# Convolution module of a two-layer trunk: the last gate ahead of the first tile's transposes, silu by pairs of blocks, and sixteen identity products behind the second tile's transposes

## The chip, the cores and the metric

The kernel runs on one core of one Trainium2 chip. The metric is the device time of one execution in microseconds (us). Changes are judged by the median over runs on the same chip.

## The reference, cut to what matters

Two layers follow each other. Each is a half-step SwiGLU FFN, a token mixer, and a second half-step FFN, all with norms before and after and a residual. The mixer of layer 0 is a causal convolution module; the change touches only this one. With 256 tokens and 1024 channels it computes:

```python
def conformer_conv_module(x, w_in, b_in, w_dw, b_dw, ln_g, ln_b, w_out, b_out):
    a, gate = jnp.split(x @ w_in + b_in, 2, axis=-1)
    h = a * jax.nn.sigmoid(gate)
    h = lax.conv_general_dilated(
        h, w_dw[:, None, :].astype(h.dtype),
        window_strides=(1,), padding=[(CONV_WIDTH - 1, 0)],
        dimension_numbers=("NWC", "WIO", "NWC"),
        feature_group_count=D_MODEL) + b_dw
    h = jax.nn.silu(layer_norm(h, ln_g, ln_b))
    return h @ w_out + b_out
```

## The kernel before

The 256 tokens are two tiles of 128 rows, t = 0 and t = 1. The 1024 channels of the convolution are four chunks of 256, c = 0 to 3. All products are done in three parts: a float32 operand is split into a high part (ACT casts it, L136) and a low part (DVE subtracts, L137), and three matmuls sum high by high, high by low and low by high (`mm3`, L139 to L142). Weights come from HBM in pieces of 512 KB on SP's queue (L127) and are split in the same way, so ACT and DVE carry a steady load of weight splits beside the module's own work.

`conv_mixer` works in these steps for each tile t and chunk c:

- `gate(t, c)`: 24 matmuls of 512 columns (`project`, L291 to L295) into a PSUM tile `mm`; DVE adds the bias (L488), ACT takes the sigmoid (L491), DVE multiplies (L493), and the result is split into `lg`.
- `conv(t, c)`: the convolution by a Fourier transform along the tokens. Six matmuls (twelve for t = 1, which needs the tile before as well) bring the chunk to the spectrum, in a PSUM tile `tr`. DVE multiplies with the taps' spectrum (five instructions, L513 to L517), the product is split into `cc`, and six matmuls bring it back into another `tr`; DVE adds the bias (L526) and takes batch statistics (L527).
- `norm(t)`: when all four chunks of a tile are there, DVE joins the statistics (L531), POOL makes the reciprocal root (L151, L155), and DVE normalises the tile in two halves (L536).
- `turn(t, z)`: the normalised tile is transposed in two halves of four blocks each (PE, L546) into two `tr` tiles. ACT applies the layer norm's gain and bias to each block (L553) and takes a sigmoid (L557), DVE multiplies (L558), and the result is split into `xt`. In the first half this goes by pairs of blocks (256 columns), in the second by all four (512).
- the output product: `expand` (L303) makes 48 matmuls of 512 columns for a tile into two `acc` tiles, and `post_norm` adds to the residual.

PSUM has four `acc` tiles, two `mm` and two `tr`; a new `tr` takes the buffer of the last but one, and its first writer waits until that one has been read. The code states the work in a program order; a scheduler decides at build time the order in which each engine's queue holds it, and fills in work that stands further down in the code. On the chip each engine runs its queue. The order around the change is this, in the code:

```python
        for t, c in ((0, 0), (1, 0), (0, 1), (1, 1), (0, 2)):
...
        sa = turn(0, za)
        conv(1, 3)
...
        sbt = turn(1, norm(1))
        accs = [[acc(), acc()] for _ in range(NT)]
        expand(accs[0], blocks(*sa, KD), wo, True, True)
        post_norm(0, accs[0], gain, 1.0, b_out)
```

The second tile's `expand` and its `post_norm` are handed on as `rest`, and run inside the start of the next FFN, whose `pre_norm` transposes the residual (L175). `behind(pe)` (L113) is a helper that makes the instructions told inside it come after the last instruction told so far on that engine.

Of the kernel before, what the change touches and what calls it, by code (L numbers as in the profile page):

```python
# [11 lines left out]
AF = mybir.ActivationFunctionType  # L12
ALU = mybir.AluOpType
# [3 lines left out]
P = 128  # L17
D = 1024
ROOT = 32.0
KD = D // P  # L20
FF = 2816
CH = 256
# [18 lines left out]
def trunk_kernel(  # L41
# [39 lines left out]
    def acc():  # L81
        return new(ps, [P, 512], F32, "acc", 4)
# [4 lines left out]
    def tr():  # L87
        return new(ps, [P, 512], F32, "tr", 2)
# [209 lines left out]
    def blocks(hi, lo, n):  # L298
        if len(hi.shape) == 3:
            return [(hi[:, k], lo[:, k]) for k in range(n)]  # L300
        return [(hi[:, k * P : (k + 1) * P], lo[:, k * P : (k + 1) * P]) for k in range(n)]
# [169 lines left out]
    def conv_mixer(layer, spectrum, before):  # L471
# [4 lines left out]
        xt = start(base, before)  # L476
        hc = [b4() for _ in range(NT)]
        stats = [new(sb, [P, 4, 6], F32, "stats", 2) for _ in range(NT)]
        glu = {}
        ws = {}  # L480

        def gate(t, c):
# [12 lines left out]
            split(hl[:, :CH], hl[:, CH:], h)  # L495
            glu[t, c] = hl

        def conv(t, c):
            sl = slice(c * CH, (c + 1) * CH)
            u = tr()  # L500
            srcs = [(glu[t, c], C_FWD)]
            if t > 0:
                srcs.append((glu[t - 1, c], C_HIS))
            for part in range(2):
                for i, (hl, off) in enumerate(srcs):
                    cs = slice(off + part * NH, off + (part + 1) * NH)
                    mm3(u[:NH, part * CH : (part + 1) * CH], dh[:, cs], dl[:, cs],
                        hl[:, :CH], hl[:, CH:], i == 0, i == len(srcs) - 1)
            wri = wspec[c // 2][:NH, c % 2 * 512 : c % 2 * 512 + 512]
            wr, wi = wri[:, :CH], wri[:, CH:]  # L510
            m1, m2 = wide("ca"), wide("cb")
            y = m1
            dve.tensor_tensor(m1[:NH], u[:NH, :], wri, op=ALU.mult)  # L513
            dve.tensor_tensor(m2[:NH, :CH], u[:NH, :CH], wi, op=ALU.mult)
            dve.tensor_tensor(m2[:NH, CH:], u[:NH, CH:], wr, op=ALU.mult)
            dve.tensor_tensor(y[:NH, :CH], m1[:NH, :CH], m1[:NH, CH:], op=ALU.subtract)
            dve.tensor_tensor(y[:NH, CH:], m2[:NH, :CH], m2[:NH, CH:], op=ALU.add)  # L517
            yh, yl = wide("cc", F32R), wide("cc", F32R)
            split(yh[:NH], yl[:NH], y[:NH])
            v = tr()  # L520
            for part in range(2):
                cs = slice(C_INV + part * P, C_INV + (part + 1) * P)
                ys = slice(part * CH, (part + 1) * CH)
                mm3(v[:, :CH], dh[:NH, cs], dl[:NH, cs], yh[:NH, ys], yl[:NH, ys],
                    part == 0, part == 1)
            dve.tensor_tensor(hc[t][:, sl], v[:, :CH], b_dw[:, sl], op=ALU.add)  # L526
            dve.bn_stats(stats[t][:, c, :], hc[t][:, sl])  # L527
# [9 lines left out]
                                  op0=ALU.subtract, op1=ALU.mult)  # L537
            return z

        def turn(t, z):  # L540
            hi, lo = turned(t)
            for h in range(2):
                pt = tr()
                for j in range(4):
                    k = h * 4 + j
                    pe.transpose(pt[:, j * P : (j + 1) * P], z[:, k * P : (k + 1) * P], ident)  # L546
                y, s = hc[t][:, h * 512 : (h + 1) * 512], z[:, h * 512 : (h + 1) * 512]
                for j in range(4):
                    k = h * 4 + j
                    js = slice(j * P, (j + 1) * P)  # L550
                    g = gcol[:, G_LN + k : G_LN + k + 1]
                    b = gcol[:, G_LN + KD + k : G_LN + KD + k + 1]
                    act.activation(y[:, js], pt[:, js], AF.Identity, scale=g, bias=b)  # L553
                step = 256 if h == 0 else 512
                for a in range(0, 512, step):
                    bs = slice(a, a + step)
                    act.activation(s[:, bs], y[:, bs], AF.Sigmoid)  # L557
                    dve.tensor_tensor(y[:, bs], y[:, bs], s[:, bs], op=ALU.mult)  # L558
                    ks = slice((h * 512 + a) // P, (h * 512 + a + step) // P)
                    split(hi[:, ks], lo[:, ks], y[:, bs].rearrange("p (k m) -> p k m", m=P))  # L560
            return hi, lo

        for t, c in ((0, 0), (1, 0), (0, 1), (1, 1), (0, 2)):
            gate(t, c)
            conv(t, c)
        gate(0, 3)
        conv(0, 3)
        za = norm(0)
        gate(1, 2)
        conv(1, 2)  # L570
        gate(1, 3)
        sa = turn(0, za)
        conv(1, 3)
        b_out = row(V_BOUT)
        gain = row(V_POST + base)
        wo = [weight(True) for _ in range(8)]
        sbt = turn(1, norm(1))
        accs = [[acc(), acc()] for _ in range(NT)]
        expand(accs[0], blocks(*sa, KD), wo, True, True)
        post_norm(0, accs[0], gain, 1.0, b_out)  # L580

# [361 lines left out]
```

## Time and profile before

| | |
|---|---|
| Median of three runs | 1009.26 us (1008.78 to 1009.34) |
| The profiled execution | 1008.88 us, of which 1007.0 us is the span from the first to the last instruction |
| PE busy | 99% of the span |
| DVE busy | 74% |
| ACT busy | 54% |
| Mean granted TensorE clock | 0.995 of full speed |

The span is what the trace shows; 1.88 us lie outside of it. PE is TensorE's matmuls, DVE is VectorE, ACT is ScalarE, POOL is GpSimd. The convolution module occupies roughly 199 to 293 us of the span.

### The profile page before, as it was taken

To read this page: it belongs to the slowest core of one execution; us is meant where nothing else is said; L and a number is where in the kernel's file an instruction comes from. 1 tells how busy PE (TensorE), PEld (TensorE's weight loads), DVE (VectorE), ACT (ScalarE), POOL (GpSimd) and SP (SyncE) were. 2 spreads that over 40 slices of the span, in tenths; PEclk is the share of its full clock that TensorE was granted. 3 is DMA by queue.
4 is the path that set the end of the run, shared out by engine and by line. 5 is a ranking of instruction groups with operands and counts; after the bars stand their busy time and mean duration, and the time that the engine had idled before them with its cause. 6 is when DMAs were issued, how large, how long until landed. Compare 5 with 4: busy or idle time off the path is not lost.

```text
span 1007.0 us, 14787 instructions
## 1 busy us (share of the span) xinstructions
PE 992.5 (99%) x5412; PEld 854.8 (85%) x5412; DVE 749.7 (74%) x1274; ACT 548.6 (54%) x1000; POOL 53.6 (5%) x93
## 2 busy tenths in 40 slices
PE   9999999999899999999999999999999999999997
PEld 7888888888778888888888888889998888888886
DVE  6877667799887776767776767687788596767673
ACT  6656545764485555455755554584143385555541
POOL 1000000010021000000200000030001120000000
PEclk9999999999899999999999999999999999999999
DMA  7885555642527564646465646465232555555541
GB/s 250 273 279 181 187 198 172 236 179 104 181 96 235 180 219 161 222 160 221 168 198 178 210 166 223 167 208 179 82 126 93 179 195 181 189 187 199 178 147 42
DMA packets 50952, 182.06 MB, mean 181 GB/s; under 512 B 6048, under 2 KB 6176, under 8 KB 50880
## 3 DMA queue, kind: packets, MB, share of 16 engines
q1 hardware_dynamic: 50736, 181.09, 53.4%
q8 instruction: 42, 0.69, 0.3%
q14 instruction: 30, 0.25, 0.1%
q10 hardware_dynamic: 144, 0.03, 0.0%
HBM read 180.06 MB, written 1.05 MB: 180 GB/s over the span
## 4 chain that ended last, share of the span: by engine, by line
PE 94%; DVE 2%; ACT 1%; DMA 1%; POOL 1%; issue 0%; DVEq 0%; POOLq 0%; SPq 0%; ACTq 0%
PE tr L331 14%; PE mm L331 14%; PE acc L141 9%; PE acc L140 9%; PE acc L142 9%; PE tr L333 7%; PE mm L333 7%; PE mm L291 4%; PE mm L292 4%; PE mm L295 4%; PE tr L654 2%; PE mm L351 2%; PE mm L352 2%; PE mm L350 2%; DMA raw<-wts 1%; PE tr L175 1%
## 5 line engine op out<-in xcount | busy, mean ns | idle before, releaser
L137 DVE TENSOR_TENSOR wl<-raw,wh 128x1024 fp32r<-128x1024 f32 (+1 forms) x386 | 399.9, 1059 | 89.1 <-ACT wh L136 65.0
L136 ACT CAST wh<-raw 128x1024 fp32r<-128x1024 f32 (+1 forms) x386 | 340.4, 921 | 124.7 <-DMA raw<-wts 72.3
L331 PE MATMUL mm<-xt,wh 128*128 128x512 f32 x640 | 161.6, 393 | 0.5 <-ACT wh L136 0.5
L331 PE MATMUL tr<-xt,wh 128*128 128x512 f32 x640 | 160.7, 392 | 0.0
L140 PE MATMUL acc<-wh,b 128*128 128x512 f32 x352 | 138.0, 392 | 0.0
L141 PE MATMUL acc<-wl,b 128*128 128x512 f32 x352 | 137.4, 390 | 0.0
L331 PEld LDWEIGHTS mm<-xt,wh 128*128 128x128 f32 x640 | 116.9, 188 | 24.1 <-ACT wh L136 1.3
L142 PE MATMUL acc<-wh,b 128*128 128x512 f32 x352 | 137.0, 389 | 0.0
L331 PEld LDWEIGHTS tr<-xt,wh 128*128 128x128 f32 x640 | 115.0, 189 | 20.7
L333 PEld LDWEIGHTS mm<-xt,wl 128*128 128x128 f32 x640 | 87.5, 190 | 6.7 <-DVE wl L137 0.4
L333 PEld LDWEIGHTS tr<-xt,wl 128*128 128x128 f32 x640 | 87.3, 190 | 6.2
L333 PE MATMUL mm<-xt,wl 128*128 128x256 f32 x640 | 90.0, 282 | 0.2 <-DVE wl L137 0.2
L333 PE MATMUL tr<-xt,wl 128*128 128x256 f32 x640 | 89.2, 282 | 0.0
L136 ACT CAST b<-e 128x256 fp32r<-128x256 f32 x80 | 32.5, 406 | 95.8 <-DVE e L412 95.8
L142 PEld LDWEIGHTS acc<-wh,b 128*128 128x128 f32 x352 | 66.1, 188 | 14.1
L140 PEld LDWEIGHTS acc<-wh,b 128*128 128x128 f32 x352 | 66.2, 188 | 12.6
L141 PEld LDWEIGHTS acc<-wl,b 128*128 128x128 f32 x352 | 66.2, 188 | 12.2
L336 ACT COPY e<-tr 128x256 f32<-128x256 f32 x80 | 29.4, 368 | 85.1 <-PE tr L333 85.1
L337 DVE TENSOR_TENSOR ga<-tr,e 128x256 f32<-128x256 f32 x80 | 33.7, 421 | 55.6 <-ACT e L336 55.6
L291 PE MATMUL mm<-wh,xt 128*128 128x512 f32 x176 | 70.0, 398 | 0.0
L292 PE MATMUL mm<-wl,xt 128*128 128x512 f32 x176 | 69.2, 393 | 0.0
L336 ACT COPY e<-mm 128x256 f32<-128x256 f32 x80 | 29.7, 371 | 49.0 <-PE mm L333 48.8
(180 smaller groups left out, 1251.9 us busy)
## 6 DMA issues: line engine op xcount, KB each, us to landing
raw<-wts SPq DMA_DIRECT2D x328, 512.0 KB, 4.8
b<-rows SPq DMA_DIRECT2D x10, 512.0 KB, 6.5
b<-x_turned SPq DMA_DIRECT2D x4, 256.0 KB, 6.3
x<-x_in SPq DMA_DIRECT2D x2, 512.0 KB, 8.4
out_dram<-x SPq DMA_DIRECT2D x4, 256.0 KB, 2.0
b<-dft SPq DMA_DIRECT2D x1, 371.0 KB, 4.8
ca<-masks SPq DMA_DIRECT2D x1, 192.0 KB, 4.5
b<-w_dw SPq DMA_DIRECT2D x1, 128.0 KB, 4.9
```

The lines of the kernel that those rows point to most:

```text
L136: act.copy(dst_h, src)
L137: dve.tensor_tensor(dst_l, src, dst_h.bitcast(F32), op=ALU.subtract)
L140: pe.matmul(o, lh, rh, start=first, stop=False)
L141: pe.matmul(o, lh, rl, start=False, stop=False)
L142: pe.matmul(o, ll, rh, start=False, stop=last)
L291: pe.matmul(o, hi[:, k], wh[:, sl], start=k == 0, stop=False)
L292: pe.matmul(o, hi[:, k], wl[:, sl], start=False, stop=False)
L295: pe.matmul(o, a, w, start=False, stop=h == 1 and n == 3)
L331: pe.matmul(pair, block(ws[k // 2][0], k), xhl[:, k], start=k == 0, stop=False)
L333: pe.matmul(pair[:, 0], block(ws[k // 2][1], k), xhl[:, k, 0], start=False, stop=k == KD - 1)
L336: act.copy(cross, o[:, SEQ:])
L337: dve.tensor_tensor(res[:, part * SEQ : (part + 1) * SEQ], o[:, :SEQ], cross, op=ALU.add)
```

## The change

Three things are edited in `conv_mixer`.

- `conv` is cut in two functions, `spectral` (to the spectrum, the product with the taps, its split) and `back` (the six matmuls back, bias, statistics). In the code `turn(0, za)` now stands behind `gate(1, 3)` and ahead of `back(1, 2)`, where before `conv(1, 2)` was told whole ahead of `gate(1, 3)`. The two DVE products of 256 columns (L514, L515) become one of 512 columns that reads the taps with the halves swapped (L513 of the changed kernel).
- In `turn` both halves go by pairs: gain and bias for two blocks, then their sigmoid, product and split, then the next two. Before, the gain and bias of all four blocks stood ahead.
- Behind the second tile's transposes sixteen products of the identity with itself are told, into `accs[1][0]`, which the second tile's `expand` overwrites later. For this the four `acc` tiles are made ahead of `turn(1, ...)`.

```diff
-        def conv(t, c):
-            sl = slice(c * CH, (c + 1) * CH)
+        def spectral(t, c):
             u = tr()
...
-            dve.tensor_tensor(m2[:NH, :CH], u[:NH, :CH], wi, op=ALU.mult)
-            dve.tensor_tensor(m2[:NH, CH:], u[:NH, CH:], wr, op=ALU.mult)
+            dve.tensor_tensor(m2[:NH].rearrange("p (s n) -> p s n", s=2),
+                              u[:NH].rearrange("p (s n) -> p s n", s=2),
+                              wri.rearrange("p (s n) -> p s n", s=2)[:, ::-1, :], op=ALU.mult)
...
             split(yh[:NH], yl[:NH], y[:NH])
+            prod[t, c] = yh, yl
+
+        def back(t, c):
+            yh, yl = prod.pop((t, c))
+            sl = slice(c * CH, (c + 1) * CH)
             v = tr()
...
-        def turn(t, z):
+        def turn(t, z, spare=None):
...
+                if spare is not None and h == 1:
+                    with behind(pe):
+                        for j in range(16):
+                            pe.matmul(spare[:, j % 4 * P : (j % 4 + 1) * P], ident, ident, start=True, stop=True)
                 y, s = hc[t][:, h * 512 : (h + 1) * 512], z[:, h * 512 : (h + 1) * 512]
-                for j in range(4):
...
-                    act.activation(y[:, js], pt[:, js], AF.Identity, scale=g, bias=b)
-                step = 256 if h == 0 else 512
-                for a in range(0, 512, step):
-                    bs = slice(a, a + step)
+                for a in range(0, 512, 256):
+                    bs = slice(a, a + 256)
+                    ks = slice((h * 512 + a) // P, (h * 512 + a + 256) // P)
+                    for j in range(a // P, a // P + 2):
...
+                        act.activation(y[:, js], pt[:, js], AF.Identity, scale=g, bias=b)
                     act.activation(s[:, bs], y[:, bs], AF.Sigmoid)
                     dve.tensor_tensor(y[:, bs], y[:, bs], s[:, bs], op=ALU.mult)
...
         za = norm(0)
         gate(1, 2)
-        conv(1, 2)
+        spectral(1, 2)
         gate(1, 3)
         sa = turn(0, za)
-        conv(1, 3)
+        back(1, 2)
+        spectral(1, 3)
+        back(1, 3)
         b_out = row(V_BOUT)
         gain = row(V_POST + base)
         wo = [weight(True) for _ in range(8)]
-        sbt = turn(1, norm(1))
         accs = [[acc(), acc()] for _ in range(NT)]
+        sbt = turn(1, norm(1), accs[1][0])
         expand(accs[0], blocks(*sa, KD), wo, True, True)
```

What the scheduler makes of it is seen at three places. The first is PE's queue at the end of `gate(1, 3)` (L295, into `mm`); `tr` from `cc` is a product back, `tr` from `ident` a transpose, `tr` from `lg` a product to the spectrum. Before:

```order
L295 MATMUL mm_2650<-wh_2507,xt 128x512 x2
L140 MATMUL tr_2641<-cc_2637,b_177_921 128x256
L546 MATMUL tr_2684<-ident,b_527_2580 128x128 x4
L141 MATMUL tr_2641<-cc_2638,b_177_921 128x256
L142 MATMUL tr_2641<-cc_2637,b_178_922 128x256
L140 MATMUL tr_2641<-cc_2637,b_177_921 128x256
L141 MATMUL tr_2641<-cc_2638,b_177_921 128x256
L142 MATMUL tr_2641<-cc_2637,b_178_922 128x256
L546 MATMUL tr_2701<-ident,b_527_2580 128x128 x4
L140 MATMUL tr_2714<-lg_2681,b_177_921 81x256
```

The same place now:

```order
L295 MATMUL mm_2634<-wh_2502,xt 128x512 x2
L551 MATMUL tr_2668<-ident,b_527_2574 128x128 x4
L551 MATMUL tr_2685<-ident,b_527_2574 128x128 x4
L140 MATMUL tr_2702<-cc_2630,b_177_921 128x256
L141 MATMUL tr_2702<-cc_2631,b_177_921 128x256
L142 MATMUL tr_2702<-cc_2630,b_178_922 128x256
L140 MATMUL tr_2702<-cc_2630,b_177_921 128x256
L141 MATMUL tr_2702<-cc_2631,b_177_921 128x256
L142 MATMUL tr_2702<-cc_2630,b_178_922 128x256
L140 MATMUL tr_2711<-lg_2665,b_177_921 81x256
```

Both groups of transposes have moved ahead of the whole of `back(1, 2)`. Its `tr_2702` now takes the buffer of the first transposes (`tr_2668`), and `spectral(1, 3)` with `tr_2711` that of the second (`tr_2685`).

The second place is PE's queue at the end of `spectral(1, 3)`. Before, the first tile's `expand` (`acc` from `wh` and `wl`) stands right behind it:

```order
L142 MATMUL tr_2714<-lg_2544,b_178_922 81x256
L140 MATMUL acc_2854<-wh_2753,xt 128x512
L141 MATMUL acc_2854<-wl_2754,xt 128x512
L140 MATMUL acc_2855<-wh_2753,xt 128x512
L142 MATMUL acc_2854<-wh_2753,xt 128x512
L141 MATMUL acc_2855<-wl_2754,xt 128x512
```

Further down its queue, 22 matmuls of the 48 stand ahead of the first matmul of `back(1, 3)` and 42 ahead of the second tile's transposes. Now:

```order
L142 MATMUL tr_2711<-lg_2539,b_178_922 81x256
L140 MATMUL tr_2734<-cc_2730,b_177_921 128x256
L141 MATMUL tr_2734<-cc_2731,b_177_921 128x256
L142 MATMUL tr_2734<-cc_2730,b_178_922 128x256
L140 MATMUL tr_2734<-cc_2730,b_177_921 128x256
L141 MATMUL tr_2734<-cc_2731,b_177_921 128x256
L142 MATMUL tr_2734<-cc_2730,b_178_922 128x256
L551 MATMUL tr_2824<-ident,b_585_2821 128x128 x4
L551 MATMUL tr_2841<-ident,b_585_2821 128x128 x4
L555 MATMUL acc_2813<-ident 128x128 x16
L140 MATMUL acc_2811<-wh_2749,xt 128x512
```

All 48 matmuls of the first tile's `expand` have moved behind `back(1, 3)`, the second tile's transposes and the sixteen identity products; the second tile's 48 follow, with the next FFN's transposes (L175) behind fifteen of them.

The third place is ACT's queue at the same point as the first. Before:

```order
L136 CAST wh_2809<-raw_2807 128x512 x2
L491 ACTIVATE e_2677<-ga_2675 128x256
L136 CAST cc_2637<-ca_2630 81x512
L136 CAST lg_2681<-e_2679 128x256
L553 ACTIVATE b_406_2064<-tr_2684,gcol 128x128 x4
L557 ACTIVATE b_527_2580<-b_406_2064 128x256 x2
```

Now:

```order
L136 CAST wh_2805<-raw_2803 128x512 x2
L565 ACTIVATE b_406_2064<-tr_2668,gcol 128x128 x2
L491 ACTIVATE e_2661<-ga_2659 128x256
L136 CAST cc_2630<-ca_2624 81x512
L566 ACTIVATE b_527_2574<-b_406_2064 128x256
L136 CAST lg_2665<-e_2663 128x256
L565 ACTIVATE b_406_2064<-tr_2668,gcol 128x128 x2
L565 ACTIVATE b_406_2064<-tr_2685,gcol 128x128
L136 CAST xt<-b_406_2064 128x2x128
L566 ACTIVATE b_527_2574<-b_406_2064 128x256
L565 ACTIVATE b_406_2064<-tr_2685,gcol 128x128 x2
L566 ACTIVATE b_527_2574<-b_406_2064 128x256
```

The reading of the transposes is now woven into the gate's and the spectrum's work; one more L565 of `tr_2685` follows. DVE's queue between `spectral(1, 3)` and the second tile's transposes holds what it held before, the weight splits among it, with the two products L514 and L515 as one.

## Rows read from the trace of the kernel before

**Rows 1.** The page's first part: busy us and share of each engine.

```profile
PE 992.5 (99%) x5412; PEld 854.8 (85%) x5412; DVE 749.7 (74%) x1274; ACT 548.6 (54%) x1000; POOL 53.6 (5%) x93
```

**Rows 2.** Busy time by stretch around the transposes, with granted clock as PEclk.

```profile
256.52:259.24 2.72, 0.01 (x1) 0.01 (x1) 2.72 (x7) 1.86 (x4) 0.00 (x0) 1.00 1.00 387
259.24:266.60 7.36, 7.18 (x30) 6.33 (x31) 6.20 (x15) 6.76 (x18) 0.00 (x0) 0.54 0.36 128
280.18:292.93 12.75, 12.18 (x56) 9.82 (x57) 11.13 (x24) 10.94 (x27) 0.85 (x2) 1.00 0.19 66
```

**Rows 3.** PE in order of time: start, us; in brackets idle before it, releaser.

```profile
255.44 1.08 PE L295 MATMUL mm<-wh,xt 128*128 128x512 f32 x4
259.24 0.39 PE L140 MATMUL tr<-cc,b 81*128 81x256 f32 x1 [2.72 <-ACT cc L136]
...
262.84 0.41 PE L141 MATMUL tr<-lg,b 128*81 128x256 f32 x1
...
264.97 0.41 PE L142 MATMUL tr<-lg,b 128*81 128x256 f32 x1
...
272.68 0.28 PE L142 MATMUL tr<-cc,b 81*128 81x256 f32 x1
...
276.67 1.11 PE L546 MATMUL tr<-ident,b 128*128 128x128 f32 x8 [0.29 <-DVE b L536]
277.54 0.47 PE L140 MATMUL acc<-wh,xt 128*128 128x512 f32 x1
...
285.12 0.66 PE L175 MATMUL tr<-ident,x 128*128 128x128 f32 x4 [0.57 <-DVE x L279]
...
286.57 0.40 PE L142 MATMUL acc<-wh,xt 128*128 128x512 f32 x1
...
292.70 0.39 PE L142 MATMUL acc<-wh,xt 128*128 128x512 f32 x1
292.93 0.39 PE L291 MATMUL mm<-wh,xt 128*128 128x512 f32 x1
...
296.66 0.66 PE L175 MATMUL tr<-ident,x 128*128 128x128 f32 x4 [0.62 <-DVE x L279]
```

**Rows 4.** DVE in order of time, at the first and the second tile's norm.

```profile
254.31 1.01 DVE L536 TENSOR_SCALAR b<-b,tiny,tiny 128x512 f32<-128x512 f32 x2 [0.71 <-POOL tiny L155]
...
255.83 0.68 DVE L513 TENSOR_TENSOR ca<-tr,b 81x512 f32<-81x512 f32 x1
256.43 0.41 DVE L514 TENSOR_TENSOR cb<-tr,b 81x256 f32<-81x256 f32 x1
256.76 0.41 DVE L515 TENSOR_TENSOR cb<-tr,b 81x256 f32<-81x256 f32 x1
...
274.87 0.25 DVE L531 BATCH_NORM_AGGREGATE tiny<-stats 128x2 f32<-128x24 f32 x1
276.07 1.00 DVE L536 TENSOR_SCALAR b<-b,tiny,tiny 128x512 f32<-128x512 f32 x2 [0.95 <-POOL tiny L155]
```

**Rows 5.** ACT in order of time, from the last weight cast to the first sigmoids.

```profile
256.32 1.14 ACT L136 CAST wh<-raw 128x512 fp32r<-128x512 f32 x2 [2.83 <-DMA raw<-wts]
258.26 0.42 ACT L491 ACTIVATE e<-ga 128x256 f32<-128x256 f32 x1 [0.80 <-DVE ga L488]
258.58 0.60 ACT L136 CAST cc<-ca 81x512 fp32r<-81x512 f32 x1
...
260.15 1.51 ACT L553 ACTIVATE b<-tr,gcol 128x128 f32<-128x128 f32 x4 [0.28 <-PE tr L546]
261.54 0.73 ACT L557 ACTIVATE b<-b 128x256 f32<-128x256 f32 x2
```

**Rows 6.** PE: identity products at the program's start, other products of their size later.

```profile
1.50 5.49 PE L202 MATMUL tr<-ident 128*128 128x128 f32 x24 [1.50 <-POOL ident masks.py:199]
...
742.59 1.05 PE L639 MATMUL tr<-b,b 128*128 128x128 f32 x8
743.40 0.48 PE L291 MATMUL mm<-wh,xt 128*128 128x512 f32 x1
```

More of the change, by code (lines that the diff above doesn't have):

```diff
@@ L478, in conv_mixer @@
         stats = [new(sb, [P, 4, 6], F32, "stats", 2) for _ in range(NT)]
-        glu = {}
+        glu, prod = {}, {}
         ws = {}
@@ L546, in turn @@
                     pe.transpose(pt[:, j * P : (j + 1) * P], z[:, k * P : (k + 1) * P], ident)
+                if spare is not None and h == 1:
+                    with behind(pe):
+                        for j in range(16):
+                            pe.matmul(spare[:, j % 4 * P : (j % 4 + 1) * P], ident, ident, start=True, stop=True)
                 y, s = hc[t][:, h * 512 : (h + 1) * 512], z[:, h * 512 : (h + 1) * 512]
-                for j in range(4):
[L549 to L552, printed above, removed]
-                    act.activation(y[:, js], pt[:, js], AF.Identity, scale=g, bias=b)
-                step = 256 if h == 0 else 512
-                for a in range(0, 512, step):
-                    bs = slice(a, a + step)
+                for a in range(0, 512, 256):
+                    bs = slice(a, a + 256)
+                    ks = slice((h * 512 + a) // P, (h * 512 + a + 256) // P)
+                    for j in range(a // P, a // P + 2):
+                        k = h * 4 + j
+                        js = slice(j * P, (j + 1) * P)
+                        g = gcol[:, G_LN + k : G_LN + k + 1]
+                        b = gcol[:, G_LN + KD + k : G_LN + KD + k + 1]
+                        act.activation(y[:, js], pt[:, js], AF.Identity, scale=g, bias=b)
                     act.activation(s[:, bs], y[:, bs], AF.Sigmoid)
                     dve.tensor_tensor(y[:, bs], y[:, bs], s[:, bs], op=ALU.mult)
-                    ks = slice((h * 512 + a) // P, (h * 512 + a + step) // P)
                     split(hi[:, ks], lo[:, ks], y[:, bs].rearrange("p (k m) -> p k m", m=P))
             return hi, lo
-        for t, c in ((0, 0), (1, 0), (0, 1), (1, 1), (0, 2)):
+        for t, c in ((0, 0), (1, 0), (0, 1), (1, 1), (0, 2), (0, 3)):
             gate(t, c)
-            conv(t, c)
-        gate(0, 3)
-        conv(0, 3)
+            spectral(t, c)
+            back(t, c)
         za = norm(0)
         gate(1, 2)
-        conv(1, 2)
+        spectral(1, 2)
         gate(1, 3)
         sa = turn(0, za)
-        conv(1, 3)
+        back(1, 2)
+        spectral(1, 3)
+        back(1, 3)
         b_out = row(V_BOUT)
```

## Prediction

> **What bounds the kernel now.** The page comes first: PE is busy for 992.5 of 1007.0 us, so nearly every microsecond at which PE stands still, or runs at the lower clock, is a microsecond of the time [rows 1]. The next view is therefore PE in order of time, searched for idle time. The largest gap behind the program's start lies inside the convolution module, where PE has finished the last gate and waits 2.72 us, up to 259.24, for the split of tile 1's spectrum [rows 3]. The windows show what follows: the granted clock averages 0.54 over the next 7.36 us, so PE runs there mostly at the lower of its two levels, 1.2 GHz instead of 2.4 [rows 2]. The reader should see from the same timeline that PE is then fed without a longer pause: the first tile's output products cover the wait for the product back of the second tile, which comes through at 272.68, and most of the wait for its norm, so that the transposes at 276.67 cost only 0.29 us of idle time [rows 3]. The stage ends for our purpose at 292.93, where the next FFN's first product starts [rows 3].
>
> **What the change moves.** I follow the new queues from the end of the gate at 256.52, 255.44 plus 1.08 [rows 3], and ask at each step which engine is last. The part ahead of it keeps its work and its order but for small swaps, and PE has no gap there that could shrink; I count it at nothing. If the swaps opened gaps there, they would come on top.
>
> *The first transposes.* The normalised tile is written from 254.31 for 1.01 us, done at 255.32 [rows 4], so the eight transposes run at once behind the gate. Eight take 277.54 - 276.67 = 0.87 us at the full clock [rows 3], so PE is through at about 257.3. That much of the 2.72 us is filled.
>
> *The product back, `back(1, 2)`.* It needs the buffer that ACT still reads. ACT is free after two weight casts that start at 256.32 and take 1.04 us of its queue, at 257.36 (steps are from one start to the next, so a little under the busy times) [rows 5]. Its queue then holds two gain-and-bias blocks at (261.54 - 260.15) / 4 = 0.35, the gate's sigmoid at 0.32, the cast of `cc` at 0.52 (the like step of a weight cast), a sigmoid at 0.31, the cast of `lg` at 0.31, and two more blocks at 0.35 [rows 5]: 0.70 + 0.32 + 0.52 + 0.31 + 0.31 + 0.70 = 2.86, and 0.1 for the last one's end. PE gets the buffer at 260.35 and has been idle for 3.05 us, 0.33 more than before. DVE's split of `cc` is ready earlier, near 259.7, since DVE meets one weight split fewer ahead of it and L514 and L515, 0.33 each, cost 0.60 together as one 512-column product like L513 [rows 4]: the saving of 0.06 in a convolution is hidden behind PE everywhere but in this chain.
>
> *The twelve products to the spectrum.* They wait for the buffer of the second transposes: ACT has a block, a cast, a sigmoid, two blocks, a sigmoid and a block still to go, 4 x 0.35 + 3 x 0.31 = 2.33 from 260.21, so they start at about 262.7. With the lower clock they step by (264.97 - 262.84) / 10 = 0.213 [rows 3] and are done at 262.7 + 11 x 0.213 + 0.41 = 265.4, as late as before (264.97 + 0.41).
>
> *The wait for `back(1, 3)`.* Here PE's queue has lost its cover. From 265.45, DVE does L512, a split of `xt` that stands in between, L513, L516, a weight split and L517: 0.60 + 0.34 + 0.60 + 0.34 + 0.60 + 0.41 = 2.89, with 256-column steps as L514's and 512-column ones as L513's [rows 4]. The cast and the way to PE take 0.66, from 258.58 to 259.24 [rows 3, 5]. The first matmul starts at 269.1. The other five need the low half, which stands behind two weight splits: 268.3 + 3 x 0.60 + 0.1 = 270.2. Six matmuls are over at about 271.5. Before, this point was 272.68 + 0.28 = 272.96 [rows 3], so tile 1's chain gains some 1.5 us, and PE has stood idle for 3.7 and 0.7 us of it, where before it made output products.
>
> *The wait for the second transposes.* From there to their start it was 276.67 - 272.96 = 3.71 us before [rows 3], with 1.20 from L531 to L536 through POOL and 0.60 for the first half of L536 in it [rows 4]. DVE's queue holds the same instructions here and three weight splits ahead, which end at 271.9; I take 3.5. The transposes start at 275.0, 1.7 earlier, but PE has idled all the way.
>
> *The identity products.* Twelve of them at the program's start are 24 records in 5.49 us, 0.229 each [rows 6]; sixteen are 32 records. Eight records of the same size elsewhere take 743.40 - 742.59 = 0.81, 0.10 each [rows 6]. So they cost between 3.2 and 7.3 us. After the long gaps I expect the lower clock at the start. Before, the low stretch lasted 7.36 us from PE's resuming [rows 2], and the slow records at the program's start 5.49 [rows 6]. I take 5.2 us here, near the second, where PE also ran without a break: transposes at half pace to 276.6, sixteen records to 280.2, sixteen at 0.11 (0.87 / 8, as the transposes) to 282.0. A low stretch of 7.4 us would give 283.1, one of only 3.4 us 281.0.
>
> *The output products.* Twenty-seven steps from 286.57 to 292.70 take 6.13 us, 0.227 each [rows 3], so 48 take 10.9. All 48 of tile 0 are now behind the identity products: 282.0 + 10.9 = 292.9. Tile 1's 48 follow with the eight transposes of the next FFN (0.95 with the slower neighbours); these need the residual 296.66 - 292.93 = 3.73 after the tile's last product, and fifteen products cover 3.40, so PE waits 0.33, no longer 0.57 [rows 3]. The next FFN starts at 292.9 + 10.9 + 0.95 + 0.33 = 305.1 against 292.93. Its second transposes stand behind twenty products, 4.54 us, and no longer wait 0.62 [rows 3].
>
> **The sum** is +12.2 - 0.6 = +11.6 us. PE is busy all through what follows, so nothing gives it back. The profiled time of 1008.88 becomes 1020.5; the median of the runs shown is 0.38 higher, so I predict 1020.7.
>
> **Where a rule is weighed.** In rows 3 PE waited 0.29 us at 276.67 with six output products behind the transposes whose operands were long there; it did not take them first. The Trainium skill, "TensorE: Matmul & The Clock Gate", section "Part 2: What happens when you issue a matmul", says that only weight loads are pulled ahead and matmuls stay in program order. By that rule the first rival below has no chance, and the trace agrees. On the clock, rows 2 and 3 show it low after a gap of 2.72 us. The same page, section "Part 1: The HAM clock gate", calls the throttled state the default, released by activity, which speaks for identity products in general. By the rule alone they could pay where idle time follows them; here the order puts 48 ready products behind them, and the sum stays that of the rows.
>
> **The rivals.**
> - *PE takes ready products past waiting ones* (faster). Then the idle time is filled again. Work left from 256.52 is 24 matmuls of 256 columns at half of 0.227 (2.7), 24 transposes at 0.109 (2.6), 96 products (21.8) and the identity's 3.5 at the full clock: 30.6 us against 36.4 (292.93 - 256.52), so -5.8 and 1003.5. The 0.29, 0.57 and 0.62 us waits with work behind them speak against it [rows 3]. It decides from the point where idle time falls under 5.8 us. In queue order the bare chains are longer: 3.05 ahead of `back(1, 2)`, 0.60 + 0.60 + 0.34 + 0.41 + 0.66 = 2.6 ahead of `back(1, 3)`, 2.5 ahead of the transposes (3.71 less two weight splits), 8.1 in all, a loss of 2.3 us even at the full clock throughout. Chance 0.03.
> - *The clock stays high, or returns at once.* The gaps are broken by short work. Then the spectrum is done a microsecond earlier, the second transposes start near 273.8, they and the identity products take 0.9 + 3.5, and tile 0's output starts at 278.2 instead of 282.0: +7.8, 1017. The clock held at 1.00 from 280.18 to 292.93, through the wait of 0.57 us [rows 2, 3]; the 2.72 us gap speaks against it. Chance 0.17.
> - *The clock returns later, or the splits in DVE's queue wait for weights still in flight.* One low stretch as long as before's 7.36 us inside the output products, or a transfer 2 us late in the queue ahead of `cc`, gives +14 to +17, 1023 to 1026. ACT did wait 2.83 us for weights here [rows 5], but ahead of this stretch. Chance 0.08.
> - *No measurable change*: the gaps would have to add up to some 4 to 8 us. Chance 0.02.
>
> **How the numbers follow.** The forecast has 0.70, with its own range of +9.5 to +13.5, 1018.6 to 1022.6. The range that should hold 8 in 10 reaches into the second and third rival: 1016.5 to 1023.5. A difference under 0.2%, 2 us, is about what a measurement of this kernel can't tell from none. Slower 0.95, same 0.02, faster 0.03.
>
> **What would show it.** In the profile after: PE goes from the gate to the eight transposes without a gap, then waits about 3 us on ACT; about 3.7 us on ACT's `cc` at 265 to 269; about 3.5 us on DVE's normalised tile at 271 to 275; no output product (L140 to L142 into `acc`) starts ahead of the identity products; the clock is low around these; and the next FFN starts near 305. I am wrong if output products fill the gaps, if the clock stays at 1.00 through them, or if the identity products take under 4 us.

## The result, and the profile after

The changed kernel took 1023.4 us (median of four runs, 1022.28 to 1025.37); the kernel before, run beside it on the same chip, took 1009.3. The ratio is 1.0138, with a 95% interval of 1.0125 to 1.0151. The change made the kernel 1.4% slower. A slowdown was forecast, to 1020.7, with a range of 1016.5 to 1023.5.

The profiled execution took 1022.39 us with a span of 1020.5. The page's first part, as [rows 1] for before:

```profile
PE 998.1 (98%) x5444; PEld 858.9 (84%) x5444; DVE 750.3 (74%) x1270; ACT 550.7 (54%) x1004; POOL 51.4 (5%) x93
```

PE is 5.6 us busier, but the span is 13.5 longer: the greater part is PE standing still. PE in order of time shows where (start, us; in brackets the idle time before it and its releaser):

```profile
256.11 1.07 PE L295 MATMUL mm<-wh,xt 128*128 128x512 f32 x4
257.02 1.36 PE L551 MATMUL tr<-ident,b 128*128 128x128 f32 x8
...
261.07 0.39 PE L140 MATMUL tr<-cc,b 81*128 81x256 f32 x1 [2.69 <-ACT b L565]
...
263.38 0.50 PE L140 MATMUL tr<-lg,b 128*81 128x256 f32 x1 [1.34 <-ACT b L565]
...
265.81 0.41 PE L142 MATMUL tr<-lg,b 128*81 128x256 f32 x1
...
269.86 0.58 PE L140 MATMUL tr<-cc,b 81*128 81x256 f32 x1 [3.63 <-ACT cc L136]
...
271.02 0.58 PE L141 MATMUL tr<-cc,b 81*128 81x256 f32 x1 [0.57 <-DVE cc L137]
...
272.04 0.41 PE L142 MATMUL tr<-cc,b 81*128 81x256 f32 x1
...
275.98 1.94 PE L551 MATMUL tr<-ident,b 128*128 128x128 f32 x8 [3.53 <-DVE b L541]
277.71 4.47 PE L555 MATMUL acc<-ident 128*128 128x128 f32 x32
...
281.94 0.47 PE L140 MATMUL acc<-wh,xt 128*128 128x512 f32 x1
...
292.93 0.39 PE L140 MATMUL acc<-wh,xt 128*128 128x512 f32 x1
...
305.38 0.39 PE L291 MATMUL mm<-wh,xt 128*128 128x512 f32 x1
...
310.47 1.32 PE L175 MATMUL tr<-ident,x 128*128 128x128 f32 x8 [0.40 <-DVE x L279]
```

Read it against [rows 3]. There, one long wait of 2.72 us, and output products (`acc<-wh`) in the later ones. Here, five waits of 2.69, 1.34, 3.63, 0.57 and 3.53 us, 11.76 in all, and not one output product among them: the first starts at 281.94, behind the sixteen identity products (L555, 32 records). The windows, with the granted clock as PEclk, show the second half of the damage:

```profile
261.07:263.38 2.31, 0.97 (x7) 0.76 (x7) 2.31 (x7) 2.31 (x8) 0.00 (x0) 0.74 0.21 67
263.38:266.20 2.82, 2.82 (x12) 2.48 (x12) 1.63 (x5) 2.82 (x8) 0.00 (x0) 0.50 0.33 131
266.20:269.86 3.66, 0.03 (x1) 0.00 (x0) 3.59 (x8) 1.09 (x2) 0.00 (x0) 0.50 0.00 0
...
275.98:277.71 1.73, 1.73 (x8) 1.73 (x9) 0.31 (x1) 0.61 (x2) 0.00 (x0) 0.50 0.56 220
277.71:281.94 4.23, 4.23 (x34) 4.23 (x33) 1.95 (x5) 4.20 (x14) 0.00 (x0) 0.82 0.00 0
281.94:292.93 10.99, 10.99 (x52) 9.10 (x51) 1.67 (x4) 0.74 (x3) 0.00 (x0) 1.00 0.00 0
...
257.18:305.38 48.20, 36.03 (x177) 30.11 (x175) 32.11 (x69) 24.42 (x64) 1.80 (x4) 0.82 0.31 106
```

The clock is at its lower level from about 262 to about 279, where before it averaged 0.54 over 7.36 us [rows 2]. The last row is the stretch from the end of the last gate to the next FFN's first product; below it is called the stage. The same row of the kernel before:

```profile
256.52:292.93 36.41, 31.65 (x144) 25.85 (x145) 29.90 (x64) 24.17 (x59) 1.59 (x4) 0.91 0.35 126
```

The first number is the length, the second PE's busy time. The stage grew by 48.20 - 36.41 = 11.79 us: PE's busy time by 4.38, with the identity products' 4.23 in it, and its idle time from 4.76 to 12.17, by 7.41.

### The profile page after: what moved, and what is told of

Same layout as the page of the kernel before. It is cut to its first block, busy times and chain, and to the rows that moved or that the text cites. A ratio compares the mean times of both kernels' runs of the same rounds, so it can differ in the third digit from the quotient of the medians.

```text
span 1020.5 us, 14869 instructions
## 1 busy us (share of the span) xinstructions
PE 998.1 (98%) x5444; PEld 858.9 (84%) x5444; DVE 750.3 (74%) x1270; ACT 550.7 (54%) x1004; POOL 51.4 (5%) x93
## 3 DMA queue, kind: packets, MB, share of 16 engines
HBM read 180.06 MB, written 1.05 MB: 177 GB/s over the span
## 4 chain that ended last, share of the span: by engine, by line
PE 90%; DVE 3%; DMA 3%; ACT 2%; POOL 1%; issue 1%; SPq 0%; DVEq 0%; POOLq 0%; ACTq 0%
PE tr L331 14%; PE mm L331 14%; PE acc L141 8%; PE acc L140 8%; PE acc L142 8%; PE tr L333 7%; PE mm L333 7%; PE mm L295 4%; PE mm L291 4%; PE mm L292 3%; DMA raw<-wts 3%; PE tr L663 2%; DVE wl L137 2%; PE mm L351 2%; PE mm L352 2%; PE mm L350 2%
## 5 line engine op out<-in xcount | busy, mean ns | idle before, releaser
L142 PEld LDWEIGHTS acc<-wh,b 128*128 128x128 f32 x352 | 66.1, 188 | 14.1
```

What stands on the lines that cost most here:

```text
L142: pe.matmul(o, ll, rh, start=False, stop=last)
```

## The experiments

The theory: the loss has two parts. One is **displacement**: the identity products, held behind the second tile's transposes, hold all 48 output products behind them, so that the waits lie bare. The other is the **identity products' own time** on PE. The rivals: the loss comes from the moved gate or from the silu by pairs; or the identity products cost their time wherever they stand. The stage and PE's busy time in it are from one profiled execution of each kernel, which can lie up to 2 us off the kernel's median (pairs_only's took 1008.22, split_only's 1010.74); the last columns are medians against the kernel before, run beside it.

| kernel | stage, us | PE busy in it | its mean clock | median, us | to before, us | ratio, 95% |
|---|---|---|---|---|---|---|
| before | 36.41 | 31.65 | 0.91 | 1009.3 to 1010.5 | | |
| after | 48.20 | 36.03 | 0.82 | 1023.4 | +14.1 | 1.0138 [1.0125, 1.0151] |
| ident_only | 49.05 | 37.54 | 0.83 | 1023.57 | +13.8 | 1.0136 [1.0122, 1.0149] |
| disp_no_ident | 45.73 | 34.19 | 0.78 | 1019.5 | +9.7 | 1.0090 [1.0076, 1.0103] |
| no_ident | 35.77 | 30.18 | 0.95 | 1010.61 | +0.8 | 1.0007 [0.9998, 1.0016] |
| no_behind | 33.28 | 32.14 | 1.00 | 1007.33 | -3.2 | 0.9969 [0.9957, 0.9981] |
| warm12 | 33.29 | 31.24 | 1.00 | 1007.18 | -2.6 | 0.9973 [0.9961, 0.9984] |
| warm12_nopairs | 33.86 | 31.20 | 1.00 | 1007.04 | -3.4 | 0.9965 [0.9953, 0.9977] |
| split_only | 36.30 | 31.71 | 0.91 | 1008.97 | -1.5 | 0.9985 [0.9976, 0.9993] |
| pairs_only | 35.48 | 30.08 | 0.95 | 1010.27 | -0.2 | 0.9993 [0.9983, 1.0002] |
| before_fill | 35.08 | 31.63 | 1.00 | 1009.4 | -0.5 | 0.9991 [0.9982, 1.0000] |
| fill_all | 43.32 | 42.88 | 1.00 | 1018.0 | +8.1 | 1.0071 [1.0058, 1.0085] |
| ident32 | 52.32 | 40.03 | 0.87 | 1026.27 | +16.4 | 1.0158 [1.0143, 1.0173] |

### Without the identity products: no_ident

```diff
-        sbt = turn(1, norm(1), accs[1][0])
+        sbt = turn(1, norm(1))
```

> The changed kernel without the sixteen identity products; the gate ahead of the transposes, the silu by pairs and the early making of the acc tiles stay. Its PE queue puts 8 output products ahead of the second tile's products to the spectrum, 23 ahead of the rest of its product back and 44 ahead of its transposes. Theory (what costs is that the output products stand behind the identity products): the waits of 3.63, 0.57 and 3.53 us on PE are covered again and the time falls under the kernel before, since the wait of 2.72 us is partly filled by eight transposes: some 27.2 us of work plus 3 us of wait plus some 2.5 us lost to the low clock against 36.4 us, so about 1006.5, range 1004.5 to 1009. Rival (the split into spectral and back, or the woven ACT queue, costs): the time stays near 1020.

The loss is gone: 1010.61, ratio 1.0007 [0.9998, 1.0016]. The split of `conv`, the moved gate and the pairs are all still there, so they are not its cause. In PE's queue the output products stand between the other work again, 8 of them ahead of the products to the spectrum and 27 ahead of `back(1, 3)`, and PE's waits of 1.3, 3.6, 0.6 and 3.5 us shrink to one of 0.36 at the transposes; the first wait stays:

```profile
261.24 0.39 PE L140 MATMUL tr<-cc,b 81*128 81x256 f32 x1 [2.68 <-ACT b L565]
...
276.40 1.06 PE L551 MATMUL tr<-ident,b 128*128 128x128 f32 x8 [0.36 <-DVE b L541]
...
280.22 0.50 PE L140 MATMUL acc<-wh,xt 128*128 128x512 f32 x1 [1.83 <-ACT xt L136]
```

The gain that I expected of it did not come: 1010.61 lies above the 1004.5 to 1009 of the expectation. The transposes fill 1.20 us behind the gate, but the wait behind them is as long as the old one, since ACT's reading of them now stands ahead of `back(1, 2)`; and the wait for `xt` is 1.83 us, where before it was 1.01:

```profile
280.18 0.50 PE L140 MATMUL acc<-wh,xt 128*128 128x512 f32 x1 [1.01 <-ACT xt L136]
```

### The displacement alone: disp_no_ident

No identity products, but the output products are told so that they must follow the second tile's transposes.

```diff
-        sbt = turn(1, norm(1), accs[1][0])
-        expand(accs[0], blocks(*sa, KD), wo, True, True)
+        sbt = turn(1, norm(1))
+        with behind(pe):
+            expand(accs[0], blocks(*sa, KD), wo, True, True)
```

> The changed kernel without the identity products, but with the first tile's output products told behind the second tile's transposes, so that PE's queue is the changed one less the identity products. Theory (the displaced output products cost, the identity products themselves little): the waits of 2.7, 1.3, 3.6, 0.6 and 3.5 us stay, the 4.23 us of identity products go, and the output products start at the low clock instead and lose about 0.85 us, so 3.4 us less than the changed kernel: 1020, range 1018.5 to 1021.5. Rival (the identity products are the main cost): the time falls to about 1010.

1019.5, as expected: +9.7 of the +14.1, with no identity product at all. The waits are those of the changed kernel, but for the second:

```profile
260.25 0.53 PE L140 MATMUL tr<-cc,b 81*128 81x256 f32 x1 [2.69 <-ACT b L565]
...
262.56 0.50 PE L140 MATMUL tr<-lg,b 128*81 128x256 f32 x1 [0.71 <-ACT b L565]
...
269.04 0.58 PE L140 MATMUL tr<-cc,b 81*128 81x256 f32 x1 [3.63 <-ACT cc L136]
...
270.20 0.58 PE L141 MATMUL tr<-cc,b 81*128 81x256 f32 x1 [0.58 <-DVE cc L137]
...
275.15 1.94 PE L551 MATMUL tr<-ident,b 128*128 128x128 f32 x8 [3.52 <-DVE b L541]
```

### The identity products alone: ident_only

The kernel before, with the sixteen identity products behind the second tile's transposes, and neither the moved gate nor the pairs.

```diff
-        def turn(t, z):
+        def turn(t, z, spare=None):
...
                     pe.transpose(pt[:, j * P : (j + 1) * P], z[:, k * P : (k + 1) * P], ident)
+                if spare is not None and h == 1:
+                    with behind(pe):
+                        for j in range(16):
+                            pe.matmul(spare[:, j % 4 * P : (j % 4 + 1) * P], ident, ident, start=True, stop=True)
...
-        sbt = turn(1, norm(1))
         accs = [[acc(), acc()] for _ in range(NT)]
+        sbt = turn(1, norm(1), accs[1][0])
```

> The kernel before with the sixteen identity products behind the second tile's transposes and the acc tiles made ahead, nothing else. Its PE queue shows the output products displaced as in the changed kernel. Theory: the 2.72 us wait stays, the waits for the product back and for the norm are bare as in the changed kernel, and the time is about 1022, range 1020 to 1024. Rival (the split or the pairs cost): only the identity products' own 4 us are added, 1013, or nothing.

1023.57, the changed kernel's time within the intervals. This one edit of the three holds the whole loss. Its waits are 2.73, 0.53, 3.96, 0.57 and 3.44 us; the third, and the products behind the last:

```profile
270.88 0.58 PE L140 MATMUL tr<-cc,b 81*128 81x256 f32 x1 [3.96 <-ACT cc L136]
...
278.67 4.66 PE L550 MATMUL acc<-ident 128*128 128x128 f32 x32
```

### The same products, free to move: no_behind

```diff
-                    with behind(pe):
+                    if True:
                         for j in range(16):
```

> The changed kernel with the sixteen identity products told at the same place in the code, but free for the scheduler to place: it puts twelve of them right behind the first tile's transposes, four behind back(1, 2), and the output products fill the waits again. Theory (the loss is the output products that stand behind all told in front of them, not the identity products as such): sixteen products that fill the 2.7 us wait behind the first transposes keep the clock at 1.00; about as warm12, 1007.2, with 0.5 us for the four that fill no wait: 1006 to 1009, ratio 0.997 to 0.9995. Rival (the identity products cost PE their 4.2 us wherever they stand): 1010.6 of the kernel without them plus 4.2, about 1014.8.

1007.33, ratio 0.9969 [0.9957, 0.9981]: the same sixteen products, told at the same place, and the kernel is faster than before. The scheduler takes twelve of them up right behind the first tile's transposes and four behind `back(1, 2)`, and the output products fill the later waits, 39 of them ahead of the second tile's transposes:

```profile
258.63 2.84 PE L555 MATMUL acc<-ident 128*128 128x128 f32 x24
...
262.28 1.05 PE L555 MATMUL acc<-ident 128*128 128x128 f32 x8
...
275.04 1.06 PE L551 MATMUL tr<-ident,b 128*128 128x128 f32 x8 [0.63 <-DVE b L541]
```

So the identity products do not cost their time wherever they stand, and this rival is out: what cost was the order that `behind` forces.

### In the first gap on purpose: warm12 and warm12_nopairs

The identity products held behind the first tile's transposes, twelve of them. warm12_nopairs also has the silu of the kernel before.

```diff
-                        for j in range(16):
+                        for j in range(12):
...
-        sa = turn(0, za)
+        accs = [[acc(), acc()] for _ in range(NT)]
+        sa = turn(0, za, accs[1][0])
...
-        accs = [[acc(), acc()] for _ in range(NT)]
-        sbt = turn(1, norm(1), accs[1][0])
+        sbt = turn(1, norm(1))
```

> The changed kernel with twelve identity products behind the first tile's transposes instead of sixteen behind the second's. They stand in the wait ahead of the product back of tile 1; the output products are not displaced. Theory on the clock (it fell since PE stood idle there): 24 records of 0.11 fill 2.6 of the about 3 us of wait, the granted clock stays at 1.00 through the stage, and the low clock's loss of about 2.5 us goes: 1004, range 1002.5 to 1006. Rival (the identity products do nothing for the clock, or it falls later anyway): the same time as without identity products, 1006.5, or slower by what they delay.

> As warm12 (twelve identity products behind the first tile's transposes, none behind the second's), but with the silu of the kernel before. Theory (the gain of warm12 is the clock that stays at 1.00; the pairs add nothing that PE waits for): as warm12, 1006 to 1008.5, ratio 0.996 to 0.999. Rival (without pairs ACT gives the transposes' buffers back in another order and back(1, 2) or the spectrum comes later than the twelve products cover): the clock falls again, 1009 to 1011.

1007.18 and 1007.04: both beat both kernels, by half of what I expected of warm12, and the pairs make no difference that the intervals could tell. In warm12 the gap is closed without a remainder:

```profile
254.93 1.07 PE L295 MATMUL mm<-wh,xt 128*128 128x512 f32 x4
255.84 1.37 PE L551 MATMUL tr<-ident,b 128*128 128x128 f32 x8
257.05 2.84 PE L555 MATMUL acc<-ident 128*128 128x128 f32 x24
259.90 0.39 PE L140 MATMUL tr<-cc,b 81*128 81x256 f32 x1
...
273.47 1.07 PE L551 MATMUL tr<-ident,b 128*128 128x128 f32 x8 [0.60 <-DVE b L541]
...
276.65 0.50 PE L140 MATMUL acc<-wh,xt 128*128 128x512 f32 x1 [0.95 <-ACT xt L136]
...
289.29 0.39 PE L291 MATMUL mm<-wh,xt 128*128 128x512 f32 x1
```

Its stage as a window (length, PE's busy time; the 1.00 near the end is the clock):

```profile
256.00:289.29 33.29, 31.24 (x169) 25.44 (x167) 29.60 (x66) 23.93 (x63) 1.59 (x4) 1.00 0.39 128
```

`back(1, 2)` comes 259.90 - 256.00 = 3.90 us behind the gate's end, as in the changed kernel (261.07 - 257.18 = 3.89): ACT sets it, with or without products in the gap (no_ident, 261.24 - 257.36 = 3.88, waits for ACT there). What the products change is the clock, 1.00 in the whole stage, and with it PE's pace behind the gap.

### The other edits alone: split_only and pairs_only

split_only is no_ident with the silu of the kernel before; pairs_only is the kernel before with gain, bias and silu of both halves by pairs, as in the changed kernel:

```diff
-                for j in range(4):
...
-                step = 256 if h == 0 else 512
-                for a in range(0, 512, step):
-                    bs = slice(a, a + step)
+                for a in range(0, 512, 256):
+                    bs = slice(a, a + 256)
+                    step = 256
+                    for j in range(a // P, a // P + 2):
...
```

> The changed kernel without identity products and with the silu of the kernel before (four blocks of gain and bias ahead in the second half); the split of conv and the moved gate stay. Theory: the idle time behind the transposes is about 2.7 us as without pairs or a little more, the output products fill the later waits, and the end of the stage is set by the second tile's chain, as in the kernel without identity products: 1008.5 to 1011, ratio 0.9995 to 1.0015. Rival (pairs are what makes the split harmless, since back(1, 2) waits for ACT's reading of the transposes): 2 us or more slower than the kernel without identity products, 1012.5 or more.

> The kernel before, with the silu by pairs in both halves and nothing else. The first output product needs the whole first half; the pairs make only the second half's first two blocks earlier, and no product waits for those in the trace of before. Theory: same, 1008.5 to 1010.5, ratio 0.999 to 1.001. Rival (the two more instructions each on ACT and DVE and their reordering delay cc or the reading of the transposes): +1 to +2 us, 1010.5 to 1012.

pairs_only is the same as before, as expected. split_only came out a little faster than expected, 0.9985 [0.9976, 0.9993], though its stage is as long as that of before (36.30). Its profile can't show where that comes from: the profiled execution, 1010.74, is the slowest of the eleven. It is also faster than no_ident, which was not run beside it, so pairs on top of the split may cost something; the wait for `xt` at the second tile's output, 1.83 us in no_ident, is 1.14 here. That is a hint and no more.

### Filling the old kernel's gap: before_fill

```diff
         gate(1, 3)
+        accs = [[acc(), acc()] for _ in range(NT)]
+        with behind(pe):
+            for j in range(12):
+                pe.matmul(accs[1][0][:, j % 4 * P : (j % 4 + 1) * P], ident, ident, start=True, stop=True)
         sa = turn(0, za)
...
-        accs = [[acc(), acc()] for _ in range(NT)]
```

> The kernel before, with twelve identity products behind the last gate, in the 2.72 us in which PE waits for cc, and no other edit. The scheduler puts eleven of them ahead of back(1, 2) and leaves the output products where they were. Theory (the gap's damage is the low clock behind it, 7.36 us at 0.54, and any work that bridges the gap keeps the clock up): the stretch at 0.54 goes to 1.00, worth 2 to 3 us: 1006.5 to 1008.5, ratio 0.9965 to 0.9985, as warm12 without the moved gate. Rival (the transposes ahead of back(1, 2), the moved gate, are what warm12's gain needs, since ACT is the last in the chain anyway): no change, 1009 to 1010.5.

A miss. The products bridge the 2.72 us to within 0.28, and the clock is 1.00 throughout, yet the median is 1009.4, 0.9991 [0.9982, 1.0000]. PE in order of time, and then the stage as a window, suggest why:

```profile
258.71 0.39 PE L140 MATMUL tr<-cc,b 81*128 81x256 f32 x1 [0.28 <-ACT cc L136]
...
260.94 0.66 PE L546 MATMUL tr<-ident,b 128*128 128x128 f32 x4 [0.41 <-DVE b L526]
...
262.13 0.34 PE L140 MATMUL tr<-lg,b 128*81 128x256 f32 x1 [0.53 <-ACT b L553]
```

```profile
255.98:291.06 35.08, 31.63 (x169) 25.63 (x168) 30.63 (x66) 23.92 (x59) 1.58 (x4) 1.00 0.40 138
```

PE's busy time is that of before (31.65): the twelve products take what the higher clock gives back. And PE, now quicker, waits 0.41 and 0.53 us for DVE and ACT where at the low clock, in the kernel before, it had waited 0.18 once:

```profile
261.71 1.12 PE L546 MATMUL tr<-ident,b 128*128 128x128 f32 x4 [0.18 <-ACT b L553]
```

The executions of the kernel before that ran beside it suggest how little the clock is worth in its order, some 1.2 us: ten of the fifteen had a mean granted clock of 0.994 to 0.996 and a median of 1010.4, five had 0.997 or 0.998 and 1009.2. before_fill, with 0.998 or 0.999 in all eleven, is no faster than those five.

With the moved gate the twelve products share the gap with eight transposes that have to be done anyway, and those two waits don't come: 33.29 against 35.08. Neither half shows a gain alone that the intervals could tell (no_ident, before_fill); together they do. So the rival that the moved gate is needed stood here, and my theory that any work in the gap will do fell. That it is those two waits that make the difference is read from one profiled execution of each kernel, and not tested by itself.

### Products in every wait: fill_all

The changed kernel with fifty identity products more. In the place of `with behind(pe)` and its loop the diff says `fill(n)`.

```diff
         gate(1, 3)
+        accs = [[acc(), acc()] for _ in range(NT)]
         sa = turn(0, za)
+        fill(12)
         back(1, 2)
+        fill(6)
         spectral(1, 3)
+        fill(16)
         back(1, 3)
+        fill(16)
...
-        accs = [[acc(), acc()] for _ in range(NT)]
```

> The changed kernel with fifty identity products more: twelve behind the first tile's transposes, six behind back(1, 2), sixteen behind spectral(1, 3), sixteen behind back(1, 3); nine output products now stand ahead of the second tile's transposes, the other 39 behind all identity products as in the changed kernel. Theory (the waits in the changed kernel cost twice, as idle time and as the low clock in the work between and behind them): 66 identity products at 0.22 are 14.4 us in the place of 11.8 us of waits and of 4.2 us for sixteen, the clock stays at 1.00, the next FFN starts near 300 instead of 305: about 1018, 1016 to 1020, ratio 1.007 to 1.010. Rival (the clock plays no part in the loss, it is idle time and products alone): fifty more products fill waits that stay as long, the time is that of the changed kernel or more, 1023 to 1028.

1018.0: fifty products more than the changed kernel, and +8.1 to before in the place of +14.1. In PE's order of time the transposes now follow without a wait, and in the stage's window PE is busy for 42.88 of 43.32 us, at 1.00:

```profile
269.23 0.39 PE L140 MATMUL tr<-cc,b 81*128 81x256 f32 x1
...
274.78 1.04 PE L551 MATMUL tr<-ident,b 128*128 128x128 f32 x8
275.66 3.74 PE L555 MATMUL acc<-ident 128*128 128x128 f32 x32
...
279.15 0.48 PE L140 MATMUL acc<-wh,xt 128*128 128x512 f32 x1
```

```profile
257.25:300.57 43.32, 42.88 (x276) 37.87 (x275) 32.05 (x69) 25.05 (x63) 1.80 (x4) 1.00 0.35 117
```

Not all of this is the clock. Nine output products stand ahead of the transposes here, and the 4.88 us by which the stage is shorter hold 9 x 0.227 = 2.0 for them [rows 3]; the other 2.8 are about what the low clock costs the changed kernel, an estimate, since DVE's queue does not hold quite the same order in the two. The rest of the excess over before, 43.32 - 36.41 = 6.9 us, is not the clock's: it is waits with useless work in them, and the last sixteen products.

### Twice the products: ident32

```diff
-                        for j in range(16):
+                        for j in range(32):
```

> The changed kernel with 32 identity products behind the second tile's transposes in the place of sixteen. Theory (by then the clock is back, so sixteen more go at 0.22 each, with every later product pushed by as much): +3.5 us, 1026 to 1028, ratio 1.016 to 1.0185. Rival (the identity products are hidden, since something else sets the start of the output products): same as the changed kernel, 1023.4.

1026.27, +16.4 to before in the place of +14.1, and +4.1 in the stage; the expected 3.5 lies between. PE in order of time, and a window of one microsecond in the first products:

```profile
277.25 8.53 PE L555 MATMUL acc<-ident 128*128 128x128 f32 x64
285.54 0.47 PE L140 MATMUL acc<-wh,xt 128*128 128x512 f32 x1
```

```profile
279.00:280.00 1.00, 1.00 (x7) 1.00 (x7) 0.76 (x2) 1.00 (x5) 0.00 (x0) 0.60 0.00 0
```

64 records take 285.54 - 277.25 = 8.29 us, where 32 took 4.23. Nothing hides them: each pushes every output product. The waits ahead are those of the changed kernel within 0.2 us.

## Why the prediction was right, and by how much it was off

**The order, and the bare waits.** Right in each step, to within 0.4 us. The stretch ahead of the stage came 0.66 us later (gate's end 257.18, not 256.52). With this taken off, `back(1, 2)` starts at 260.41 (forecast 260.35), the spectrum's products at 262.72 (262.7), `back(1, 3)` at 269.20 and its second matmul at 270.36 (269.1 and 270.2), the transposes at 275.32 (275.0). The waits were summed from ACT's and DVE's rows, and the releasers in the trace are the ones named. The first wait is 2.69 us and not 3.05, since the eight transposes end 1.20 us behind the gate and not 0.87; that changes nothing behind it. The rule of the Trainium skill that stood beside the first rival ("TensorE: Matmul & The Clock Gate", section "Part 2: What happens when you issue a matmul": matmuls stay in program order) has the trace's agreement in the four waits behind the first: PE idled 9.07 us with 48 output products queued behind. no_ident shows that operands of some were there, since it made 8 of them in the second of these places and 27 ahead of `back(1, 3)`. The first wait, 2.69 us, shows nothing of it: no_ident waits there as long.

**The identity products.** Mis-sized, and in the kernel's favour. With the transposes ahead I forecast 7.0 us (275.0 to 282.0), with the low clock for 5.2 of them; it was 281.94 - 275.98 = 5.96, with the low clock for some 3.3, to 279.3. The start that the forecast has at 282.0 is 281.28 on the corrected scale, close to the 281.0 that went with the shortest low stretch considered; for that length the prediction gave no row. The products from 277.71 to 281.94 took 4.23 us, near the 4 us under which the prediction called itself wrong. The output products' 10.9 came out at 10.99, and the next FFN started at 304.72 on the corrected scale against 305.1.

**The saving of 0.6** at the next FFN's second transposes did not come: they wait 0.40 us behind twenty products, where I forecast none. They start 5.09 us behind the FFN's first product, where before it was 3.73 and I let it stay so. The second tile's squares on ACT (L273), which the residual needs, now start at 306.21 behind a weight cast of 1.05 us and have another (306.83) between their halves; before they stood at 293.24 and 293.87, with none between. The delay against the kernel before is +12.45 at the FFN's first product and still +12.41 behind these transposes (its 25th, 312.56 against 300.15).

**What was counted at nothing.** The span grew by 13.5: 0.66 ahead of the stage, 11.79 in it, and about 1.05 behind it, 0.70 of it busy time of PE and 0.35 idle (the largest new wait is 0.38 us, at 489.01). My sum had 12.2 for the stage, 0.6 off behind it, and nothing for the other two. It was also added up 0.2 too low: 1008.88 + 11.6 + 0.38 is 1020.9, not 1020.7. The median lies at +14.1, 1023.4, above the forecast's own range (1018.6 to 1022.6) and inside the wide one by 0.1 us. The account of the stage is right; that the median still falls inside the range is luck. Whether the terms ahead and behind belong to the change stays open: in the table the stage's difference and the median's differ by 2.3 us here, and by up to 1.4 in either direction for the other kernels (split_only -0.1 and -1.5, no_ident -0.6 and +0.8).

**The rivals.** The second (clock high, 1017) fell: the clock was at 0.50 for most of the time from 262 to 279. fill_all, which holds it high by force, took 1018.0. What the clock takes is thus the smaller part, by the estimate above about 2.8 us of 11.8. The third rival (the clock back later, 1023 to 1026) had the median's number, but not in the profiled execution, where the clock was back ahead of the output products and they ran at 1.00. The four executions leave it open for the others: 1022.28 and 1022.39 had a mean granted clock of 0.990, 1024.42 and 1025.37 one of 0.988. But in ident32 three at 0.988 (1025.64, 1025.73, 1027.71) stand around one at 0.993 (1026.81), so the clock alone does not order the times.

**The cause, as the runs settle it.** ident_only has the loss without the other two edits, no_ident has the other two without the loss, disp_no_ident has two thirds of it with the displacement alone, no_behind has the products without the displacement and is faster than before. The rest, 14.1 - 9.7 = 4.4 with intervals of some 1.3 us on either side, goes with the products themselves, 4.23 us in the trace. The two profiled stages differ by less, 48.20 - 45.73 = 2.47: without the identity products the first output products run at the low clock in their place (it is back at about 280.8 there, 5.7 us behind the start of the transposes at 275.15). By these two readings the products' net share is some 2.5 to 4.4 us.

## What to carry to other kernels

Work put in to keep an engine busy must stand where the engine waits. Held by an order behind work that comes late, it takes the waits' filling with it: here sixteen useless products moved 48 useful ones. Ask of each forced order what is queued behind it, and what that work had been filling until now. A gap is worth filling when the work in it is work that has to be done anyway, or when what follows runs faster for it than the fill costs; before_fill and warm12 have the same twelve products and the same clock, and only the one that also moves the transposes into the gap gains.

## What the runs showed of the hardware that was not expected

- The lower clock ended at different times behind the same queue. PE's instructions in the changed kernel and in ident32 are the same up to the sixteenth identity product, the waits ahead agree within 0.2 us, and the clock was back some 3.3 us behind the start of the second transposes in the one (0.76 in 279.0 to 279.5) and some 4.3 in the other (0.60 in 279.0 to 280.0, transposes at 275.52). In disp_no_ident, with output products in the place of the identity products, it was 5.7 us. A microsecond more at half the clock is half a microsecond of PE's work, so the stages of single executions are uncertain by at least that much.
- The clock stayed at 0.50 through PE's work from 263.38 to 266.20 and from 269.86 to 272.45, with waits of 3.6 and 3.5 us around it; before, with output products in these waits, it was back at the end of the 7.36 us in which it averaged 0.54 [rows 2]. This fits the Trainium skill, "TensorE: Matmul & The Clock Gate", section "Part 1: The HAM clock gate", by which the lower rate is the default and activity releases it.
- An identity product of 128 columns takes two records, and sixteen took 3.5 us from start to start at the full clock (279.15 - 275.66 in fill_all, where the next product starts at 279.15): 0.22 each, about the 0.227 of an output product of 512 columns [rows 3]. As filler they are as dear as useful work of four times the columns.
